# The delta rule's small substitution on GpSimd instead of VectorE, in a hybrid decoder layer

## The chip, the cores and the metric

The kernel runs on one core of one Trainium2 chip. A core has five engines that take their instructions in order and wait for one another by semaphores: TensorE (PE; its weight loads are shown apart as PEld), VectorE (DVE), ScalarE (ACT), GpSimd (POOL) and SyncE (SP), which here issues nearly all transfers. The metric is the time of one execution on the device in microseconds, as the median of several runs. The median before is 2311.64 us.

## The reference, cut to what matters

One decoder layer on 1,024 tokens of width 1,024, in float32: a gated feed-forward layer, a mixer of eight gated delta-rule heads (head dimension 128) beside sixteen state-space heads, a second feed-forward layer, and a last norm. The change lies in the delta rule. There the reference solves a unit lower triangular system for each chunk:

```python
def gated_delta_rule(q, k, v, g, beta):
    ...
    kk = jnp.einsum("bhcld,bhcsd->bhcls", k, k)
    a_low = jnp.where(strict, beta[..., :, None] * kk * decay, 0.0)
    t_inv = lax.linalg.triangular_solve(
        eye + a_low, jnp.broadcast_to(eye, a_low.shape),
        left_side=True, lower=True, unit_diagonal=True)
    u = jnp.einsum("bhcls,bhcsd->bhcld", t_inv, v * beta[..., None])
    w = jnp.einsum("bhcls,bhcsd->bhcld", t_inv, k * (beta * jnp.exp(gc))[..., None])
    ...
```

Everything else (projections, convolutions, gates, the state that is carried from chunk to chunk) is as usual for such layers.

## The kernel before, in words

The kernel keeps full float32 accuracy on TensorE by splitting each large operand into a high and a low part and making three products (`mm3`, L121 to L123). The feed-forward layers use a one-level Strassen scheme (L332 to L334 for the first two matrices, L551 to L553 for the third). Between them stands the mixer: first the state-space heads in four units, then the eight delta-rule heads in the loop `for h in range(GH)`, then the output projection.

One pass of that loop works on 1,024 tokens as 8 blocks of 128:

- Two weight tiles of 256 columns (loaded at L147 and L148, split at L136 and L137) give q, k, v and z by projections of 24 matmuls per half (`proj_half`, three PSUM banks tagged `pj`). `conv_silu` writes each projection to the single buffer `pre`, whose first three columns GpSimd sets to zero (L775), and VectorE adds three taps (L783).
- The decay `dt` is loaded, masked by GpSimd (`causal`, L894) and exponentiated by ScalarE. TensorE makes kk and qk (L1140, L1141), and VectorE scales them into `u` and `dt` (L1144 to L1154).
- `u` is 8 blocks of 128 by 128. Its diagonal blocks of 32 by 32, 32 of them, go to DRAM (L1160) and come back as `fu` (L1194), one small block per partition, four times over, so that each of 128 partitions holds one block and a quarter of its right-hand sides. `fx` starts as that quarter of the identity (GpSimd, L1198 and L1200).
- The substitution runs over 31 columns. For column j, L1204 multiplies up to eight entries of the solution with the rest of the row into `ft`, and L1206 subtracts `ft` from `fx`. That makes 62 instructions of 8 to 76 elements per partition, each of which needs the one before.
- `fx` goes to DRAM (L1209) and comes back transposed into `lv` (L1216) and onto the diagonal of `u` (L1217). A VectorE transpose (L1218) follows, then TensorE builds the inverse of the 64 and the 128 blocks from the small ones (L1224 to L1250). GpSimd clears a part of the buffer for that (L1235). `fu`, `fx`, `ft` and `lv` have one buffer each; the tile of L1235 shares the buffer of `fu`.
- The recurrence goes through the 8 blocks: TensorE (L1273, L1278, L1283, L1284, L1287) and VectorE (`rr` L1275, `vn` L1280, `sn` L1292) in turn, ScalarE takes the outputs (L1295). The results are normalised (L1301 to L1305) and stored to `mix_scr` (L1306).

The source writes one head after the other. The order on each engine is laid by the framework (Tile) when the kernel is built, by its own estimates of how long each instruction takes; on the chip each engine keeps that order. So in the trace the projections of one head stand between the matmuls of the recurrence of the head before, and the substitution's instructions stand between VectorE's other work. SyncE's queue of transfers and GpSimd's queue are ordered in the same way.

After the loop the output projection adds four groups of state-space rows (`group_tile`, L1340 and L1342) and then two pairs of delta-rule groups (`pair_tile`). The first groups are prepared and multiplied while the last head is still at work.

The lines of the substitution:

```python
            for j in range(31):
                r, n = j // 4 + 1, 31 - j
                t = ft[:, 0:r * n].rearrange("p (s l) -> p s l", l=n)
                V.tensor_tensor(out=t, in0=fx[:, 0:r, j:j + 1].to_broadcast([P, r, n]),
                                in1=fu[:, j:j + 1, j + 1:32].to_broadcast([P, r, n]), op=ALU.mult)
                V.tensor_tensor(out=fx[:, 0:r, j + 1:32], in0=fx[:, 0:r, j + 1:32], in1=t, op=ALU.subtract)
```

`V` is VectorE, `A` ScalarE, `G` GpSimd and `T` TensorE.

Of the kernel before, what the change touches and what calls it, by code (L numbers as in the profile page):

```python
# [16 lines left out]
ALU = mybir.AluOpType  # L17
# [4 lines left out]
P = 128  # L22
# [22 lines left out]
def kernel(  # L45
# [7 lines left out]
    V, A, G, T = nc.vector, nc.scalar, nc.gpsimd, nc.tensor  # L53
# [755 lines left out]
    with tc.tile_pool(name="gtmp", bufs=1, side="right", reuse_waits="tile") as tp:  # L809
# [23 lines left out]
        for b in range(NB):  # L833
# [12 lines left out]
                        in1=bias.unsqueeze(1).to_broadcast([P, NB, NG]), op=ALU.add)  # L846
# [11 lines left out]
        for c in (15, 13, 11, 9, 7, 5, 3):  # L858
# [8 lines left out]
                               in1=alog.unsqueeze(1).to_broadcast([P, NB, NG]),  # L867
# [11 lines left out]
                        op=ALU.subtract)  # L879
# [19 lines left out]
    for un in range(4):  # L899
# [37 lines left out]
        for b0 in range(0, NB, 2):  # L937
# [6 lines left out]
            for name, lst, sc in (("xdt", xdts, bc2(dtn, b0)), ("xe", xes, bc2(dxe, b0))):  # L944
                t = s1.tile([P, 2, 256], F32, name=name, tag=name, bufs=4)
                last_x = V.tensor_tensor(out=t.rearrange("p i (h c) -> p i h c", h=4), in0=ptv, in1=sc,
                                         op=ALU.mult)
# [42 lines left out]
        for b0 in range(0, NB, 4):  # L990
# [33 lines left out]
            for b, py, *_ in pairs:  # L1024
                for j in range(2):
                    xv = xst[j][:, b * P:(b + 2) * P]
                    V.scalar_tensor_tensor(out=xv, in0=xv, scalar=dcol[:, 2 * un + j:2 * un + j + 1],
                                           in1=py[:, j * 256:(j + 1) * 256], op0=ALU.mult, op1=ALU.add)
# [71 lines left out]
    with ExitStack() as cg:  # L1100
        g1 = cg.enter_context(tc.tile_pool(name="gdn1", bufs=1, reuse_waits="tile"))
        g2 = cg.enter_context(tc.tile_pool(name="gdn2", bufs=2, reuse_waits="tile"))
        for h in range(GH):
# [31 lines left out]
            for b0 in range(0, NB, 2):  # L1135
# [14 lines left out]
                for i in range(2):  # L1150
# [4 lines left out]
                                in0=pg.rearrange("p (i c) -> p i c", i=2)[:, :, P:2 * P],  # L1155
                                in1=dt[:, b2], op=ALU.mult)
# [24 lines left out]
            for half in range(2):  # L1181
                pt = psum("mx")
                for i in range(4):
# [4 lines left out]
                                in1=rin[:, hb].unsqueeze(2).to_broadcast([P, 4, P]), op=ALU.mult)  # L1188
# [6 lines left out]
            fx = g1.tile([P, 8, 32], F32, name="fx")  # L1195
# [5 lines left out]
            for j in range(31):  # L1201
                r, n = j // 4 + 1, 31 - j
                t = ft[:, 0:r * n].rearrange("p (s l) -> p s l", l=n)
                V.tensor_tensor(out=t, in0=fx[:, 0:r, j:j + 1].to_broadcast([P, r, n]),  # L1204
                                in1=fu[:, j:j + 1, j + 1:32].to_broadcast([P, r, n]), op=ALU.mult)
                V.tensor_tensor(out=fx[:, 0:r, j + 1:32], in0=fx[:, 0:r, j + 1:32], in1=t, op=ALU.subtract)  # L1206
            fs_q = fs_x.rearrange("j b (i q) l -> q (j b) i l", q=4)
            for q in range(4):
                nc.sync.dma_start(out=fs_q[q], in_=fx[32 * q:32 * q + 32])  # L1209
# [47 lines left out]
            for half in range(2):  # L1257
                pt = psum("sc")
                for i in range(4):
# [4 lines left out]
                                in1=wend[:, hb, h:h + 1].to_broadcast([P, 4, P]), op=ALU.mult)  # L1264
# [3 lines left out]
            for b in range(NB):  # L1268
                bs = slice(b * P, (b + 1) * P)
                rr = vr[:, b]  # L1270
                if st is not None:
# [4 lines left out]
                                           in1=vr[:, b], op0=ALU.mult, op1=ALU.add)  # L1276
# [8 lines left out]
                if b < NB - 1:  # L1285
# [5 lines left out]
                    else:  # L1291
                        V.scalar_tensor_tensor(out=sn, in0=st, scalar=egt[:, b, h:h + 1],  # L1292
                                               in1=p3[:, 0:P], op0=ALU.mult, op1=ALU.add)
# [191 lines left out]
```

## Time and profile before

| | |
|---|---|
| median of 3 runs | 2311.64 us (2310.7 to 2312.34) |
| the profiled execution | 2312.76 us, of which the span of the profile is 2310.9 us |
| granted TensorE clock | 0.998 |
| HBM traffic | 211.55 MB read, 67.73 MB written, 121 GB/s over the span |
| GpSimd in the whole kernel | 53.5 us busy, 125 instructions |

A row of a group of instructions reads: line, engine, operation, output tile <- input tiles, shapes, count, then busy time and mean nanoseconds of one, then the idle time of the engine before them and what ended it. A row in order of time begins with the start and the length. A row of waits reads: who waited <- for whom, total us, times, the longest. A row of stages reads: the stretch, its length, then busy us and instructions of PE, PEld, DVE, ACT and POOL, the granted clock, the share of the DMA engines and GB/s.

### The profile page before, as it was taken

The page shows a single profiled execution, that of the slowest core. Times are in us where ns is not written, and L with a number is a line of the kernel's source. Part 1 is how long each engine was busy: PE and PEld are TensorE (multiplying, and loading weights), DVE is VectorE, ACT ScalarE, POOL GpSimd, SP SyncE. Part 2 cuts the span into 40 slices and gives each one's busy share as a digit, 9 for nine tenths or more (in the row PEclk, how much of TensorE's full clock was granted, in tenths as well). Part 3 has the DMA queues.
Part 4 walks back from the last instruction along what each step waited for, and adds up shares of the span by engine and source line. Part 5 has one row for each costly group of instructions (what it writes and reads, how often), then busy time and mean ns, then how long its engine had stood idle before and what let it go on. Part 6 is the DMA issues. An engine that isn't in the chain of part 4 may idle for free.

```text
span 2310.9 us, 31493 instructions
## 1 busy us (share of the span) xinstructions
PE 2279.0 (99%) x11766; PEld 1871.6 (81%) x11766; DVE 1726.6 (75%) x3349; ACT 1097.1 (47%) x1990; POOL 53.5 (2%) x125
## 2 busy tenths in 40 slices
PE   7999999999999999999999999999999999999998
PEld 5788888888878888888888888888878888888886
DVE  7977776767765675678778888778698777767787
ACT  7433333343467785864455556422543333334344
POOL 0000000000000100000000000000000000000000
PEclk9999999999999999999999999999999999999999
DMA  3333332573652222222333222335223333329446
GB/s 111 126 113 104 105 107 99 177 278 128 222 182 75 92 92 72 73 88 74 83 101 82 73 82 61 116 98 192 91 74 123 110 104 106 105 89 356 139 154 214
DMA packets 220957, 281.33 MB, mean 122 GB/s; under 512 B 47008, under 2 KB 153564, under 8 KB 219780
## 3 DMA queue, kind: packets, MB, share of 16 engines
q1 hardware_dynamic: 220548, 279.23, 36.8%
q8 instruction: 92, 1.51, 0.3%
q14 instruction: 61, 0.50, 0.1%
q0 software_dynamic: 256, 0.10, 0.0%
HBM read 211.55 MB, written 67.73 MB: 121 GB/s over the span
## 4 chain that ended last, share of the span: by engine, by line
PE 91%; DVE 4%; ACT 3%; issue 1%; DMA 1%; SPq 0%; POOL 0%; DVEq 0%; ACTq 0%
PE ps_pj L123 10%; PE ps_pj L121 10%; PE ps_pj L122 10%; PE ps_pj L334 6%; PE ps_pj L332 6%; PE ps_pj L333 6%; PE ps_mx L332 3%; PE ps_mx L333 3%; PE ps_mx L334 3%; PE ps_pj L552 2%; PE ps_pj L553 2%; PE ps_pj L551 2%; PE ps_oo L334 2%; PE ps_oo L333 2%; PE ps_oo L332 2%; PE ps_sc L551 1%
## 5 line engine op out<-in xcount | busy, mean ns | idle before, releaser
L123 PE MATMUL ps_pj<-hhi,wlo 128*128 128x512 f32 x832 | 334.9, 403 | 0.0
L121 PE MATMUL ps_pj<-hhi,whi 128*128 128x512 f32 x832 | 333.3, 401 | 0.4 <-ACT gsb L825 0.4
L122 PE MATMUL ps_pj<-hlo,whi 128*128 128x512 f32 x832 | 332.5, 400 | 0.0
L332 PE MATMUL ps_pj<-bh,ah 128*128 128x512 f32 x688 | 268.3, 391 | 3.0 <-ACT ah L239 1.6
L334 PE MATMUL ps_pj<-bh,al 128*128 128x512 f32 x688 | 268.8, 391 | 0.5 <-DVE al L240 0.5
L333 PE MATMUL ps_pj<-bl,ah 128*128 128x512 f32 x688 | 268.4, 390 | 0.0
L121 PEld LDWEIGHTS ps_pj<-hhi,whi 128*128 128x128 f32 x832 | 157.2, 189 | 28.7 <-ACT gsb L825 0.9
L123 PEld LDWEIGHTS ps_pj<-hhi,wlo 128*128 128x128 f32 x832 | 157.1, 189 | 28.6 <-issue 0.7
L122 PEld LDWEIGHTS ps_pj<-hlo,whi 128*128 128x128 f32 x832 | 157.0, 189 | 28.1
L332 PEld LDWEIGHTS ps_pj<-bh,ah 128*128 128x128 f32 x688 | 129.4, 188 | 30.9 <-ACT m L341 2.1
L239 ACT CAST ah<-wst 128x512 fp32r<-128x512 f32 x88 | 54.6, 622 | 209.1 <-PE ps_oo L333 124.3
L239 ACT CAST hid<-hraw 128x1024 fp32r<-128x1024 f32 (+1 forms) x84 | 82.3, 981 | 149.2 <-PE ps_oo L553 56.0
L334 PEld LDWEIGHTS ps_pj<-bh,al 128*128 128x128 f32 x688 | 129.6, 188 | 27.5 <-DVE al L240 0.9
L333 PEld LDWEIGHTS ps_pj<-bl,ah 128*128 128x128 f32 x688 | 129.6, 188 | 27.3 <-DVE bl L240 0.4
L315 DVE TENSOR_TENSOR as<-wst 128x512 f32<-128x512 f32 x220 | 145.0, 683 | 1.9 <-DMA wst<-in_ffn_w_up_dram 1.5
L240 DVE TENSOR_TENSOR al<-as,ah 128x512 fp32r<-128x512 f32 x220 | 140.9, 684 | 4.3 <-ACT ah L239 4.0
L332 PE MATMUL ps_mx<-bh,ah 128*128 128x512 f32 x352 | 138.3, 395 | 2.4 <-ACT bh L239 0.9
L333 PE MATMUL ps_mx<-bl,ah 128*128 128x512 f32 x352 | 138.4, 393 | 0.4 <-DVE bl L240 0.4
L334 PE MATMUL ps_mx<-bh,al 128*128 128x512 f32 x352 | 137.6, 391 | 0.0
L239 ACT CAST ah<-as 128x512 fp32r<-128x512 f32 x220 | 124.9, 618 | 19.2 <-DVE as L315 19.1
L240 DVE TENSOR_TENSOR hid<-hraw,hid 128x1024 fp32r<-128x1024 f32 (+1 forms) x84 | 95.0, 1131 | 33.7 <-ACT hid L239 33.0
L341 ACT COPY m<-ps_pj 128x512 f32<-128x512 f32 x88 | 51.6, 589 | 124.3 <-PE ps_pj L334 122.2
(448 smaller groups left out, 5116.7 us busy)
## 6 DMA issues: line engine op xcount, KB each, us to landing
hraw<-hid_scr SPq DMA_DIRECT2D x70, 512.0 KB, 4.3
hid_scr<-hs SPq DMA_DIRECT2D x110, 256.0 KB, 2.2
wst<-in_ffn_w_down_dram SPq DMA_DIRECT2D x50, 512.0 KB, 4.6
wst<-in_ffn_w_gate_dram SPq DMA_DIRECT2D x22, 1024.0 KB, 5.5
wst<-in_ffn_w_up_dram SPq DMA_DIRECT2D x22, 1024.0 KB, 5.2
wst<-in_w_in_dram SPq DMA_DIRECT2D x36, 512.0 KB, 5.1
hid_scr<-sg SPq DMA_DIRECT2D x44, 256.0 KB, 2.0
keep<-in_ffn_w_down_dram SPq DMA_DIRECT2D x20, 512.0 KB, 6.2
```

The source lines that it names most:

```text
L121: T.matmul(o, lhsT=wh, rhs=mh, start=first, stop=False)
L122: T.matmul(o, lhsT=wh, rhs=ml, start=False, stop=False)
L123: T.matmul(o, lhsT=wl, rhs=mh, start=False, stop=last)
L239: return (A.copy(out=hi, in_=src), V.tensor_tensor(out=lo, in0=src, in1=hi.bitcast(F32), op=ALU.subtract))
L240: V.tensor_tensor(out=lo, in0=src, in1=hi.bitcast(F32), op=ALU.subtract))
L315: V.tensor_tensor(out=t, in0=v[0], in1=v[1], op=v[2])
L332: T.matmul(bank, lhsT=wh[:, k], rhs=bh[:, k], start=a, stop=False, skip_group_check=True)
L333: T.matmul(bank, lhsT=wh[:, k], rhs=bl[:, k], start=False, stop=False, skip_group_check=True)
L334: T.matmul(bank, lhsT=wl[:, k], rhs=bh[:, k], start=False, stop=z, skip_group_check=True)
L341: A.copy(out=t, in_=bank)
L551: T.matmul(bank, lhsT=hh, rhs=wh, start=first and k == 0, stop=False, skip_group_check=True)
L552: T.matmul(bank, lhsT=hh, rhs=wl, start=False, stop=False, skip_group_check=True)
```

## The change

The two instructions of each step of the substitution are given to GpSimd. Operands, shapes, buffers and the number of instructions stay; the neighbours of the loop stay where they were.

```diff
             for j in range(31):
                 r, n = j // 4 + 1, 31 - j
                 t = ft[:, 0:r * n].rearrange("p (s l) -> p s l", l=n)
-                V.tensor_tensor(out=t, in0=fx[:, 0:r, j:j + 1].to_broadcast([P, r, n]),
+                G.tensor_tensor(out=t, in0=fx[:, 0:r, j:j + 1].to_broadcast([P, r, n]),
                                 in1=fu[:, j:j + 1, j + 1:32].to_broadcast([P, r, n]), op=ALU.mult)
-                V.tensor_tensor(out=fx[:, 0:r, j + 1:32], in0=fx[:, 0:r, j + 1:32], in1=t, op=ALU.subtract)
+                G.tensor_tensor(out=fx[:, 0:r, j + 1:32], in0=fx[:, 0:r, j + 1:32], in1=t, op=ALU.subtract)
```

## The prediction

> **What bounds the kernel now.** I read the page first, then the table by stage, then the waits of the mixer, then the order of time around one substitution.
>
> ```profile
> span 2310.9 us, 31493 instructions
> PE 2279.0 (99%) x11766; PEld 1871.6 (81%) x11766; DVE 1726.6 (75%) x3349; ACT 1097.1 (47%) x1990; POOL 53.5 (2%) x125
> ...
> PE 91%; DVE 4%; ACT 3%; issue 1%; DMA 1%; SPq 0%; POOL 0%; DVEq 0%; ACTq 0%
> ```
>
> TensorE is busy 99% of the span and is 91% of the chain that ended last. The eight heads of the delta rule lie between 976 and 1560 us (columns: length, then busy time of each engine with its count, granted clock, DMA share):
>
> ```profile
> 976.00:1560.00 584.00, 582.10 (x3808) 476.85 (x3803) 462.39 (x1437) 293.43 (x660) 24.08 (x79) 1.00 0.31 86
> ...
> PEld ps_oo L1284 <- DVE vn L1280: 8.6, 44, 0.4
> PEld ps_sc L1278 <- DVE rr L1275: 8.0, 41, 0.3
> PEld ps_sc L1273 <- DVE sn L1292: 7.4, 37, 0.4
> ...
> PEld ps_sc L1224 <- DVE lv L1218: 1.0, 3, 0.4
> ```
>
> Of 584.0 us TensorE is busy 582.1, so 1.9 us are open. The finer waits are weight loads held up by VectorE's recurrence results: 8.6 + 8.0 + 7.4 = 24.0 us in 122 waits of some 0.2 us, mostly latency from one engine to the next. L1224, the first TensorE work that uses the substitution, waits 1.0 us in all: TensorE arrives there when the data does.
>
> The moved work, all heads together:
>
> ```profile
> L1206 DVE TENSOR_TENSOR fx<-fx,ft 128x60 f32<-128x60 f32 (+24 forms) x248 | 52.5, 212 | 5.2
> L1204 DVE TENSOR_TENSOR ft<-fx,fu 128x60 f32<-128x60 f32 (+24 forms) x248 | 51.8, 209 | 5.4
> ```
>
> VectorE loses 104.3 us, 13.0 per head. It isn't the bound, so that is no time by itself. What counts is when the substitution ends. One head in order of time (start, length):
>
> ```profile
> 1201.64 1.71 SPq L1194 DMA_DIRECT2D fu<-fs_u  x4
> DMA to landing us min/median/max: 2.2/2.6/2.9
> 1212.34 0.18 DVE L1204 TENSOR_TENSOR ft<-fx,fu 128x31 f32<-128x31 f32 x1
> 1241.84 0.17 DVE L1206 TENSOR_TENSOR fx<-fx,ft 128x8 f32<-128x8 f32 x1
> 1242.08 2.53 SPq L1209 DMA_DIRECT2D fs_x<-fx  x4
> 1249.00 0.45 SPq L1216 DMA_DIRECT2D lv<-fs_x  x1
> 1252.71 0.45 DVE L1218 STREAM_TRANSPOSE lv<-lv 128x256 f32<-128x256 f32 x1
> 1253.55 0.21 PE L1224 MATMUL ps_sc<-lv,u 32*32 32x32 f32 x1
> 1259.80 1.14 PE L1250 MATMUL ps_sc<-u,lv 64*64 64x64 f32 x16
> 1268.16 1.70 SPq L1194 DMA_DIRECT2D fu<-fs_u  x4
> ```
>
> The last of four loads of `fu` is issued near 1202.9 and lands 2.6 us later, at 1205.5. VectorE gets to the substitution at 1212.3, since the recurrence of the head before and the convolution come first, and ends at 1242.0: 36.5 us after the data. Then come the trip through DRAM (L1209, L1216), the transpose at 1252.7 and TensorE at 1253.6. The last L1216, landing like the L1209 and L1194 transfers some 1.8 to 2.6 us after its issue, is there near 1250.8, so about 1.9 us are spare. The substitution may therefore take 36.5 + 1.9 = 38.4 us from the landing without TensorE noticing, if its order stays.
>
> **The change part by part.** Removed from VectorE: 62 instructions per head. Added to GpSimd: the same 62, each needing the one before. The loop gives 1,560 elements per row for each of the two kinds, a mean of 50 per instruction. The trace has no GpSimd instruction with two inputs; the nearest rows:
>
> ```profile
> L1200 POOL MEMSET fx<- 32x8 f32 x32 | 3.4, 106 | 1.8
> L82 POOL TENSOR_SCALAR_AFFINE_SELECT triu<-triu 128x128 f32<-128x128 f32 x1 | 0.3, 296 | 0.0
> ...
> 906.37 1.10 POOL L894 TENSOR_SCALAR_AFFINE_SELECT md<-md 128x1024 f32<-128x1024 f32 x1 [28.96 <-ACT cte L975]
> 977.78 0.58 POOL L1200 MEMSET fx<- 32x8 f32 x4
> ```
>
> A select of 128 elements takes 0.296 us and one of 1,024 takes 1.10, so 0.90 ns per element on a fixed 0.18 us. Four memsets of 0.106 take 0.58, so some 0.05 us lie between two instructions. At 50 elements a one-input instruction would cost 0.18 + 0.045 + 0.05 = 0.28 us: the low end, 17.4 us per head. Two inputs at twice the price make 0.45 + 0.05 = 0.50: the high end, 31.0 us. Neither is nearer, so I take the middle, 0.39 us, 24.2 us per head.
>
> The Trainium skill, GPSIMD Engine Reference, section "Elementwise — side-by-side cycle accounting", speaks against the change: a two-input instruction takes 1.96 times VectorE's time there (for 2,048 elements). By that, as an estimate, 62 instructions at 0.21 us become 25.5 us. No run here shows it yet.
>
> GpSimd doesn't run alone. In the trace:
>
> ```profile
> 1228.88 0.16 DVE L118 SCALAR_TENSOR_TENSOR co<-rs_t,co 128x8 f32<-128x8 f32 x1
> 1230.43 1.27 DVE L783 SCALAR_TENSOR_TENSOR kt<-pre,cols,kt 128x1024 f32<-128x1024 f32 x1
> 1230.66 2.00 POOL L894 TENSOR_SCALAR_AFFINE_SELECT dt<-dt 128x1024 f32<-128x1024 f32 x1 [16.68 <-PE ps_pj L123]
> 1231.63 1.05 DVE L118 SCALAR_TENSOR_TENSOR co<-rs_t,co 128x8 f32<-128x8 f32 x1
> ```
>
> The select issued during a convolution tap lasts 2.00 us instead of 1.10, and the tiny L118 behind the tap lasts 1.05 instead of 0.16, to the end of the select: they take turns. The Trainium skill, SBUF — State Buffer, section "Who interferes with whom", states it as a rule: a VectorE instruction with two SBUF inputs and a GpSimd instruction that reads SBUF block one another for the whole instruction. By that rule, the trace agrees.
>
> So each large VectorE instruction with two SBUF inputs stands in the way of the chain. Between the landing and the present end:
>
> ```profile
> L783 DVE SCALAR_TENSOR_TENSOR qt<-pre,cols,qt 128x1024 f32<-128x1024 f32 x3 | 3.8, 1281 | 0.5 <-ACT qt L781 0.5
> L783 DVE SCALAR_TENSOR_TENSOR kt<-pre,cols,kt 128x1024 f32<-128x1024 f32 x3 | 3.8, 1275 | 0.0
> L783 DVE SCALAR_TENSOR_TENSOR vt__10675<-pre,cols,vt__10675 128x1024 f32<-128x1024 f32 x2 | 2.6, 1282 | 0.0
> L137 DVE TENSOR_TENSOR wlo<-wst,whi 128x1024 fp32r<-128x1024 f32 x2 | 2.4, 1221 | 0.0
> ...
> L1305 DVE TENSOR_TENSOR vr<-vr,co 128x1024 f32<-128x1024 f32 x1 | 1.2, 1217 | 0.0
> L1129 DVE TENSOR_TENSOR qe<-qe,qt 128x1024 f32<-128x1024 f32 x1 | 1.2, 1216 | 0.0
> ```
>
> They sum to 3.8 + 3.8 + 2.6 + 2.4 + 1.2 + 1.2 = 15.0 us. GpSimd's own select and two memsets add 1.3. The recurrence's rr, vn and sn read PSUM for one input; I cost the collision there at nothing, and if that fails each of some 22 results per head waits up to 0.39 us, 8.6 us per head.
>
> With the present order of the other engines the substitution takes 24.2 + 15.0 + 1.3 = 40.5 us from the landing and ends at 1246.0, 4.0 us later than now. Less 1.9 spare, TensorE waits 2.1 us per head, 16.8 us over eight. From the ends of the price: 17.4 us and no collision end at 1224.2, early, at no cost; 31.0 us with all collisions end at 1252.8, and 8.9 us in eight heads make 71 us.
>
> But the order will be laid anew at build time, by prices I don't know. If the new order counts the 24.2 + 1.3 us of GpSimd and nothing of the turns, it expects the end near 1231 and lays L1224 and what follows 11 us earlier. Up to there VectorE's taps for q and k and one `wlo` (3.8 + 3.8 + 1.2 = 8.8 us) stand in the way; the chain is 8.8 us late, 6.9 beyond the spare, and TensorE, strictly in its order, waits that long in seven heads: 48.3 us. (The last head has fewer such instructions ahead of it.) I take the middle of 16.8 and 48.3, 32.6 us.
>
> Other queues. SyncE's L1209 now waits for GpSimd; behind it stand L1216, L1217, the store of `zc` and a load of weights:
>
> ```profile
> 1250.53 0.39 SPq L147 DMA_DIRECT2D wst<-in_w_in_dram  x1
> ...
> 1289.31 1.04 ACT L136 CAST whi<-wst 128x1024 fp32r<-128x1024 f32 x1
> ```
>
> These weights are split 38 us after their issue, so some us of delay there are hidden. On GpSimd the memsets of `pre` (L775) and the select (L894) stand among the 62; one instruction of 0.39 us ahead of them is hidden, because three `pj` banks hold two half projections of 24 matmuls ahead. L1235 need not wait for VectorE any more; nothing waited for it. The buffer `fu`, single, is held from 1201.6 to 1260.9 and refilled at 1268.2: 7.2 us of slack, so the ring bites only beyond 43.7 us.
>
> What it may gain: part of the 24.0 us of small waits and the 1.9 us open. The 62 instructions are mixed into only the later part of each recurrence; I take 4 us, at most 6 with the open time, as the bound, and 2 us as likely.
>
> The sum against the profiled execution: 2310.9 span and 1.9 around it are 2312.76 us; 2312.8 + 32.6 = 2345.4. The median of the runs is 1.1 us below that execution, so 2344.
>
> **The rivals.** First, on the other side: GpSimd is in time. It starts 6.8 us earlier than VectorE does (1205.5 against 1212.3). At 38.4 us or less from landing to end, or if the new order lays L1224 later by what GpSimd needs, TensorE just works on something else: its work is the same and there is always another head's projection. At 0.28 us an instruction, 17.4 + 15.0 + 1.3 = 33.7 us is in time. For it: the 99%, and TensorE's order that meets its data within 1.0 us today, so the order's prices are good for VectorE. Against it:
>
> ```profile
> ACT dt L1128 <- POOL dt L894: 6.1, 4, 2.4
> ```
>
> ScalarE waits for GpSimd's select in four heads, 6.1 us: where GpSimd is in the chain today, the order comes out too early. Result 2306 to 2313, likeliest 2310.
>
> Second, far slower: the order prices a GpSimd instruction like VectorE's, 0.24 us from start to start, 15 us per head, and expects the end at 1220.5. The chip needs 24.2 + 8.8 = 33 us, to 1238.5; 18.0 late, 16.1 beyond the spare, in seven heads 113 us: 2425. The memsets of `pre` would then also be late by more than the banks hide. It decides as soon as the expected price is under two thirds of the real one.
>
> **How the numbers follow.** A measurement of this kernel tells about 0.2%, 4.6 us, from no change. The forecast (a few us lost per head) gets 0.50; GpSimd in time 0.37, of which 0.07 gains more than 4.6 us and 0.30 stays within; the far slower case 0.13. So faster 0.07, same 0.30, slower 0.63. The range runs from 2308, inside the in-time case, to 2400, above the 71 us of the dear end; it leaves out part of the gain and the far slower case. The forecast's own range is 2315 to 2383.
>
> **What would show it.** Right: L1204 and L1206 on POOL at 0.3 to 0.5 us, with lengths above 1 us where a tap or `wlo` runs; waits of PEld at L1224 (or of L1218 for its load) of 2 to 7 us per head; TensorE's busy share in 976 to 1560 falling to some 95%; VectorE's busy time down by about 104 us. Wrong: L1224 without waits and the stage as long as now (in time); POOL instructions under 0.28 or over 0.50 us without a collision; waits of rr, vn or sn on POOL; a loss outside the eight heads.

## The result, and the profile after

The changed kernel takes 2466.19 us (median of 5 runs, 2462.11 to 2469.53), the kernel before on the same chip 2311.75 us. The ratio is 1.0664, with a 95% interval of 1.0652 to 1.0676: 154 us slower, where the prediction had said 32 us and at most 88. The profiled execution took 2466.19 us; its span is 2464.5 us.

The page of the changed kernel, engines and the chain that ended last:

```profile
PE 2329.3 (95%) x11766; PEld 1910.8 (78%) x11766; DVE 1647.7 (67%) x2853; ACT 1080.7 (44%) x1980; POOL 247.4 (10%) x621
...
PE 72%; POOL 8%; DVE 8%; DMA 5%; issue 3%; ACT 3%; SPq 2%; POOLq 0%; DVEq 0%; ACTq 0%
```

TensorE still has 11,766 instructions. Of the 153.6 us by which the span grew, 103.3 are idle TensorE (135.2 us idle against 31.9), and 50.3 are TensorE being busy for longer with the same work. TensorE's share of the last chain fell from 91% to 72%; GpSimd, VectorE and transfers take 21% of it, against 5% before.

The stages (same columns as before), before the heads, in them and after them:

```profile
0.00:976.00 976.00, 957.57 (x4671) 785.98 (x4672) 698.07 (x1031) 510.02 (x868) 29.80 (x48) 1.00 0.39 127
976.00:1713.00 737.00, 632.58 (x3788) 516.05 (x3787) 383.79 (x951) 278.08 (x653) 217.59 (x575) 0.87 0.25 71
1713.00:2464.50 751.50, 739.11 (x3310) 608.72 (x3309) 565.81 (x872) 292.59 (x460) 0.00 (x0) 1.00 0.42 140
```

The whole loss is in the heads: they take 737 us instead of 584, at a granted clock of 0.87 instead of 1.00. The two other stages are as long as they were. In the waits, two things stand out:

```profile
PE ps_sc L1224 <- DVE lv L1218: 87.8, 8, 13.4
DVE vt__8521 L783 <- POOL pre L775: 15.4, 1, 15.4
```

L1224 waited 1.0 us in all; now TensorE stands there in every head, some 11 us at a time. And in seven heads the taps of v wait 8 to 15 us (the longest is shown) for the memset of `pre`, which stands behind the 62 instructions on GpSimd.

Counted from the landing of its data, the substitution does not end later. One head in order of time (start, length), with the beginning of the next:

```profile
1167.07 0.39 PE L1140 MATMUL ps_mx<-kt 128*128 128x128 f32 x2
1189.25 0.24 POOL L1204 TENSOR_TENSOR ft<-fx,fu 128x31 f32<-128x31 f32 x1 [44.47 <-DMA fu<-fs_u]
1193.99 1.15 POOL L1206 TENSOR_TENSOR fx<-fx,ft 128x52 f32<-128x52 f32 x1
1198.53 0.29 POOL L1206 TENSOR_TENSOR fx<-fx,ft 128x48 f32<-128x48 f32 x1
1221.78 0.21 POOL L1206 TENSOR_TENSOR fx<-fx,ft 128x8 f32<-128x8 f32 x1
1222.02 2.52 SPq L1209 DMA_DIRECT2D fs_x<-fx  x4
1222.30 3.93 DVE L783 SCALAR_TENSOR_TENSOR vt__9957<-pre,cols,vt__9957 128x1024 f32<-128x1024 f32 x3 [12.44 <-POOL pre L775]
1232.80 0.45 DVE L1218 STREAM_TRANSPOSE lv<-lv 128x256 f32<-128x256 f32 x1 [6.58 <-DMA lv<-fs_x]
1233.30 0.26 PE L1224 MATMUL ps_sc<-lv,u 32*32 32x32 f32 x1 [11.62 <-DVE lv L1218]
1251.96 0.38 PE L1140 MATMUL ps_mx<-kt 128*128 128x128 f32 x2
1267.07 1.81 SPq L1160 DMA_DIRECT2D fs_u<-u  x4
1274.78 0.24 POOL L1204 TENSOR_TENSOR ft<-fx,fu 128x31 f32<-128x31 f32 x1 [47.69 <-DMA fu<-fs_u]
1307.07 0.21 POOL L1206 TENSOR_TENSOR fx<-fx,ft 128x8 f32<-128x8 f32 x1
1318.45 0.26 PE L1224 MATMUL ps_sc<-lv,u 32*32 32x32 f32 x1 [11.49 <-DVE lv L1218]
```

From the landing of `fu` to the end of the last L1206 it takes 32.7 us (1189.25 to 1221.99). With VectorE it took 36.5, since VectorE began 6.8 us after the landing; the 62 instructions alone took 29.7 there, so GpSimd is 3 us longer on them and still ends sooner. What changed is what lies around it. In the kernel before, TensorE started the kk products (L1140) of this head and of the next one here:

```profile
1182.49 0.38 PE L1140 MATMUL ps_mx<-kt 128*128 128x128 f32 x2
1246.79 0.38 PE L1140 MATMUL ps_mx<-kt 128*128 128x128 f32 x2
```

The second is 6.8 us ahead of L1224 (1253.55), and five of the next head's eight kk products come ahead of it. After the change none does: the first L1140 comes 18.7 us behind L1224 (1251.96 against 1233.30). So the heads have become one ring, in which the next substitution cannot begin until the one before is used: L1224 to the next kk product 18.7 us, to the store of `u` 15.1, to the first L1204 7.7, the 62 instructions 32.5, transfers to L1224 11.2. The sum is 85.2 us, the distance of two L1224 (1233.30 to 1318.45); before it was 63.2 (1253.55 to 1316.79).

The clock, in four short stretches of that head:

```profile
1222.00:1224.00 2.00, 0.00 (x0) 0.00 (x0) 1.67 (x2) 0.00 (x0) 0.26 (x2) 0.88 0.14 21
1226.00:1228.00 2.00, 0.00 (x0) 0.00 (x0) 0.22 (x1) 1.06 (x1) 0.83 (x6) 0.50 0.92 256
1248.00:1252.00 4.00, 4.00 (x19) 3.49 (x18) 1.33 (x3) 0.50 (x3) 0.00 (x0) 0.65 0.00 0
1252.00:1256.00 4.00, 4.00 (x30) 3.69 (x29) 3.30 (x8) 3.15 (x8) 0.00 (x0) 1.00 0.33 133
```

TensorE stopped near 1221.7 and went on at 1233.3. The clock fell to 0.50 in the pause and was back at 1.00 near 1250.8 (that is what a mean of 0.65 from 1248 to 1252 says), after 17.5 us of work at half speed. Over the eight heads this stretch is 8 to 18 us long, 122 us together. If all of that work ran twice as fast at the full clock, half of it, 61 us, would be extra time; 50.3 us of longer busy time were found, with the same instructions.

### The profile page after: what moved, and what is told of

Same layout as the page of the kernel before. It is cut to its first block, busy times and chain, and to the rows that moved or that the text cites. A ratio compares the mean times of both kernels' runs of the same rounds, so it can differ in the third digit from the quotient of the medians.

```text
span 2464.5 us, 31445 instructions
## 1 busy us (share of the span) xinstructions
PE 2329.3 (95%) x11766; PEld 1910.8 (78%) x11766; DVE 1647.7 (67%) x2853; ACT 1080.7 (44%) x1980; POOL 247.4 (10%) x621
## 4 chain that ended last, share of the span: by engine, by line
PE 72%; POOL 8%; DVE 8%; DMA 5%; issue 3%; ACT 3%; SPq 2%; POOLq 0%; DVEq 0%; ACTq 0%
PE ps_pj L123 7%; PE ps_pj L122 7%; PE ps_pj L121 7%; PE ps_pj L332 6%; PE ps_pj L334 6%; PE ps_pj L333 6%; POOL fx L1206 4%; POOL ft L1204 3%; PE ps_mx L332 3%; PE ps_mx L333 3%; PE ps_mx L334 3%; DMA wst<-in_ffn_w_down_dram 2%; PE ps_pj L552 2%; PE ps_pj L553 2%; PE ps_pj L551 1%
## 5 line engine op out<-in xcount | busy, mean ns | idle before, releaser
L121 PE MATMUL ps_pj<-hhi,whi 128*128 128x512 f32 x832 | 342.4, 412 | 15.6 <-ACT vt__11393 L781 3.2
L123 PE MATMUL ps_pj<-hhi,wlo 128*128 128x512 f32 x832 | 344.4, 414 | 0.0
L122 PE MATMUL ps_pj<-hlo,whi 128*128 128x512 f32 x832 | 340.7, 410 | 0.0
L121 PEld LDWEIGHTS ps_pj<-hhi,whi 128*128 128x128 f32 x832 | 162.2, 195 | 48.1 <-ACT vt__11393 L781 3.6
L1204 POOL TENSOR_TENSOR ft<-fx,fu 128x60 f32<-128x60 f32 (+24 forms) x248 | 98.2, 396 | 337.3 <-DMA fu<-fs_u 318.5
```

What stands on the lines that cost most here:

```text
L121: T.matmul(o, lhsT=wh, rhs=mh, start=first, stop=False)
L122: T.matmul(o, lhsT=wh, rhs=ml, start=False, stop=False)
L123: T.matmul(o, lhsT=wl, rhs=mh, start=False, stop=last)
L1204: G.tensor_tensor(out=t, in0=fx[:, 0:r, j:j + 1].to_broadcast([P, r, n]), in1=fu[:, j:j + 1, j + 1:32].to_broadcast([P, r, n]), op=ALU.mult)
```

## The experiments

Two theories. **Order and queues**: GpSimd is fast enough; the loss comes from what the build-time order puts behind the substitution, on TensorE and in the queues of GpSimd, SP and ScalarE. **Speed**: 62 dependent instructions on GpSimd, in turns with VectorE, are too long for a head in any order. Each run below has the range that its theory gave beforehand. The table gives every run; the period is a quarter of the distance between the first substitution instruction of heads 3 and 7 of the eight, the length is that from the first of the 62 to the end of the last, as the median of those heads; both in us, from one profile each.

| run | us | ratio to before (95%) | period | length | clock |
|---|---|---|---|---|---|
| before | 2312 | | 63.3 | 28.4 | 0.998 |
| changed kernel | 2466.2 | 1.065 to 1.068 | 84.6 | 32.5 | 0.960 |
| e3_pre_on_vector | 2469.7 | 1.066 to 1.070 | 84.4 | 32.2 | 0.959 |
| e4_no_taps | 2436.8 | 1.051 to 1.056 | 78.9 | 26.5 | 0.966 |
| e7_longer_pre_vector | 2468.5 | 1.064 to 1.070 | 83.2 | 48.2 | 0.970 |
| e1_late2 | 2423.6 | 1.046 to 1.050 | 78.4 | 28.4 | 0.979 |
| e2_late1 | 2420.5 | 1.044 to 1.049 | 77.3 | 29.6 | 0.975 |
| e5_late1_pre_vector | 2420.5 | 1.045 to 1.049 | 77.3 | 29.3 | 0.977 |
| e8_late2_pre_vector_dt | 2436.4 | 1.050 to 1.058 | 81.2 | 30.2 | 0.971 |
| e9_uncoupled | 2393.0 | 1.033 to 1.037 | 73.2 | 27.3 | 0.981 |
| e11_queues_open | 2344.4 | 1.013 to 1.016 | 65.7 | 33.1 | 0.993 |
| e6_v_late1 | 2313.8 | 0.999 to 1.001 | 64.1 | 31.0 | 0.999 |
| e10_uncoupled_vector | 2313.5 | 1.000 to 1.002 | 64.4 | 24.2 | 0.999 |
| e12_queues_open_vector | 2312.2 | 0.999 to 1.001 | 65.0 | 31.2 | 0.999 |

**e1_late2 and e2_late1: TensorE's order moved later.** The loop body becomes a generator, and what follows the substitution of a head is traced behind the first part of the next head (e2), or behind the first convolution of the head after that (e1). A `yield` lets the source of another head come in between. The diff is e2's, whose two `yield`s stand ahead of `fs_x` and ahead of `lv`; e1 has a third one behind the first convolution, and an order edge (`issue_after`) that makes the framework lay the rest of a head behind a given instruction.

```diff
-        for h in range(GH):
+        def head(h):
...
+            yield
...
+        for h in range(GH):
+            next(heads[h])
+            if h:
+                next(heads[h - 1], None)
+            next(heads[h])
```

> GpSimd substitution, with the source rearranged so that each head's work behind the substitution (from L1218 on) is laid on TensorE behind the first half of the q projection two heads later: the number of projection matmuls ahead of the second head's L1224 goes from 1513 to 1584 (1548 before the change). Order theory (the loss is TensorE reaching L1224 some 11 us before the data, and the slow clock after that wait): waits at L1224 under 10 us in all, clock at 0.99 or more, time 2305 to 2325. Rival 'GpSimd is too slow' (chain and turns themselves cost the time): the same 62 instructions and the same turns, time stays above 2400. Rival 'queue' (the memsets of pre stand behind the chain and hold up the convolution of v): the 8 to 15 us waits of the taps for pre stay, time 2340 to 2400.

> The same rearrangement with less shift: the work behind the substitution is traced just after the next head's first part, which puts the second head's L1224 behind 1536 projection matmuls instead of 1513 (23 x 0.227 = 5 us, and some kk and qk matmuls). Order theory: waits of 3 to 6 us per head instead of 11, time 2360 to 2410, between the change and e1_late2. Rival 'GpSimd is too slow': above 2440, since nothing of GpSimd's work changes.

e1 ran 99 us above the range of the order theory, into the one given for a GpSimd that is too slow; e2 ran 10 us above its range. The wait at L1224 did go (two heads of eight are left with it), but others took its place. e1, waits:

```profile
PE ps_mx L1147 <- DVE jd L1151: 66.2, 12, 9.4
ACT qe L1132 <- DMA dt<-g_scr: 79.5, 6, 13.8
```

e2, order of time near the end of one substitution (1196.89):

```profile
1203.77 1.06 ACT L1125 ACTIVATE qe<-dt 128x1024 f32<-128x1024 f32 x1 [14.19 <-DMA dt<-g_scr]
1212.98 0.79 PE L121 MATMUL ps_pj<-hhi,whi 128*128 128x512 f32 x1 [11.23 <-ACT vt__9712 L781]
1220.62 0.38 PE L1140 MATMUL ps_mx<-kt 128*128 128x128 f32 x2
```

TensorE now stands in the projections of v, whose banks ScalarE has not emptied, and the kk product still comes 24 us behind the end of the substitution. The ring has another link, but it is a ring. At first I took the memset of `pre`, in GpSimd's queue behind the 62, for that link, and passed over the first of these rows; e5 below shows the error.

**e3_pre_on_vector: the memset alone.** `G.memset(pre[:, 0:3], 0.0)` becomes `V.memset`.

> As the change, but the memset of pre (L775) made by VectorE, so that no convolution waits for GpSimd's queue; TensorE's order is the same as in the change. Order theory: the 11 us waits at L1224 stay (perhaps 1 us shorter, the memset no longer waiting inside the chain), only the 2 to 3 us waits of L121 for the v projection go: 2425 to 2455. Rival 'queue': most of the loss goes, below 2370.

No gain. In the order of the change the memset's lateness is not the wait that ends last; L1224 still waits, in these seven heads and 10.8 us in the other:

```profile
PE ps_sc L1224 <- DVE lv L1218: 79.9, 7, 15.1
```

**e4_no_taps: the substitution without most turns.** The three taps of the convolutions in the eight heads are left out (that part of the computation is missing).

> As the change, but the three taps of the convolutions of q, k and v are left out in the eight heads (VectorE's 1.28 us instructions with two SBUF inputs; the output is then another). About six of nine collisions of the chain go, 0.9 us each. Order theory with the turns as what the order leaves out: chain 26 to 27 us instead of 32.7, waits at L1224 of 4 to 6 us per head, time 2370 to 2410. Order theory with an underpriced single instruction: waits stay at 9 to 11 us, time above 2430.

```profile
1184.41 0.24 POOL L1204 TENSOR_TENSOR ft<-fx,fu 128x31 f32<-128x31 f32 x1 [4.06 <-DMA fu<-fs_u]
1208.30 0.21 POOL L1206 TENSOR_TENSOR fx<-fx,ft 128x8 f32<-128x8 f32 x1
```

Here the 62 take 24.1 us in the same head, 8.6 us less than the 32.7 above. Two of them still last 1.33 and 1.15 us beside a large VectorE instruction, so the turns are worth some 10 us a head and not only 8.6. With most of them gone, 29 us of the 154 go (some of it because the convolutions are shorter too), and L1224 still waits 76.7 us in eight heads. So the turns are not the main cause. Of the two branches of the expectation it is the second that came true, the time above 2430 us and waits of 9 to 11 us a head (9.6 here): it speaks for an order that counts too little for a single GpSimd instruction, though no run shows the order's own prices.

**e7_longer_pre_vector: a longer chain.** An idle memset of 336 columns goes ahead of each L1204 on GpSimd. (The memset of `pre` stays on GpSimd, whatever the label says.)

```diff
+                G.memset(ft, 0.0)
                 G.tensor_tensor(out=t, in0=fx[:, 0:r, j:j + 1].to_broadcast([P, r, n]),
```

> The changed kernel with an idle memset of 336 columns ahead of each product on GpSimd and the memset of pre left where it is. The chain gets some 31 x 0.35 = 11 us longer, and the order made at build time, which counts it, lays TensorE's work behind the substitution 23 to 36 projection matmuls later. Theory (TensorE's order is laid for too short a chain, and what is behind the substitution then stands in front of the next head's kk product): period of a head = kk product to the end of the wait (23 + 43 + 11 = 77 us) and almost nothing ahead of the next kk product, 78 us against 84.5 now: about 2415 to 2440 us, faster than the changed kernel although the chain is longer. Rival (the length of the chain alone sets the period): 8 x 11 us more, 2540 to 2570 us.

Both ranges were missed, but the pair of numbers says much: the substitution is 16 us longer and the kernel no slower. One head, from the first kk product of the next:

```profile
1319.42 0.38 PE L1140 MATMUL ps_mx<-kt 128*128 128x128 f32 x2
1331.60 0.26 PE L1225 MATMUL ps_sc<-lv,u 32*32 32x32 f32 x1 [8.31 <-DVE lv L1219]
1348.42 1.81 SPq L1160 DMA_DIRECT2D fs_u<-u  x4
```

The order, which counts the memsets, lays three of the next head's eight kk products ahead of the inverse (L1225) and five behind it. From the first matmul of the inverse to the next store of `u` it is 16.8 us (1331.60 to 1348.42), against 33.8 in the change (1233.30 to 1267.07). So the order takes 17.0 us out of the ring, about what the longer chain puts in (47.7 us for the substitution that follows against 32.5). The expectation had the chain 5 us too short, and 23 us from the first kk product to the substitution where it is 37 (1319.42 to 1356.72), since the wait now stands in the middle of the kk products. The length of the substitution alone does not set the time.

The clock came back sooner here, after 4.5 us of work behind the wait of 8.31 us:

```profile
1331.60:1336.00 4.40, 4.40 (x41) 3.21 (x41) 3.43 (x12) 0.81 (x2) 0.00 (x0) 0.50 0.61 186
1336.20:1340.00 3.80, 3.80 (x75) 3.23 (x74) 1.45 (x7) 1.23 (x3) 0.00 (x0) 1.00 0.53 134
```

**e5_late1_pre_vector and e6_v_late1.** e2 with the memset of `pre` on VectorE, and the rearranged order of e2 with the substitution on VectorE.

> This joins two edits that each failed alone: the work behind a head's substitution is laid on TensorE behind the next head's projections (as in e2_late1), and the memset of pre is made by VectorE, so that the convolution of v no longer queues on GpSimd behind the 62 instructions. Theory (the loop): in e2_late1 the period of a head, some 78 us, is a loop: chain end, memset of pre, convolution of v, first kk product of the next head, products and both transfers (24 us), chain (30 us). With the memset on VectorE that loop is cut; what is left is kk product to first matmul behind the substitution, 24 + 30 + 12 = 66 us, against about 64 us of TensorE's own work in the head. Then 2315 to 2345 us, waits of TensorE on ps_pj below 2 us a head, and a granted clock above 0.985. Rival (GpSimd's 62 instructions are simply too slow for a head, whatever the order): 2400 to 2425 us, with the wait moved to a third place.

> Control: the rearranged trace order of e2_late1 with the substitution still on VectorE. Every theory expects that the rearrangement alone moves little: 2305 to 2325 us. If it comes out near 2400, the loss of e2_late1 is the rearrangement's and not GpSimd's.

The control came out as before: the rearrangement is free. e5 gained nothing on e2 and lies in the range given for the rival; the trace shows the next link. The queue of SP, ScalarE and TensorE in one head (the substitution ends at 1200.50):

```profile
1200.53 2.54 SPq L1210 DMA_DIRECT2D fs_x<-fx  x4
1203.17 0.54 SPq L1124 DMA_DIRECT2D dt<-g_scr  x1
1207.10 1.06 ACT L1125 ACTIVATE qe<-dt 128x1024 f32<-128x1024 f32 x1 [14.13 <-DMA dt<-g_scr]
1216.31 0.80 PE L121 MATMUL ps_pj<-hhi,whi 128*128 128x512 f32 x1 [11.17 <-ACT vt__9712 L781]
```

SP issues in order: the store of `fx` waits for GpSimd, and the load of the next head's decay stands behind it. ScalarE, in order too, stands 14 us at the exponential of that decay, with the copies that free TensorE's banks behind it.

**e8_late2_pre_vector_dt.** The order of e1, the memset on VectorE, and the decay's load and exponentials traced ahead of the substitution.

> The later order of e1_late2 (the work behind the substitution of head h stands behind the first convolution of head h+2's projections), the memset of pre on VectorE, and the load of dt with its exponentials and its select issued ahead of the previous head's substitution instead of behind it, so that neither the SP queue nor GpSimd's queue holds the decay matrix until the chain has ended. Theory (the loop): no loop of more than about 64 us a head is left, so 2300 to 2325 us, clock above 0.99, waits behind the substitution only in the last two heads (13 us together as in e1_late2). Rival (GpSimd too slow in any order): 2400 us or more.

This one, too, landed in the rival's range. The load was traced earlier and still laid behind the store on SP. The likely reason is that its tile has two buffers and in this order the second comes free late; no run shows that alone:

```profile
1210.50 2.54 SPq L1226 DMA_DIRECT2D fs_x<-fx  x4
1216.92 0.45 SPq L1116 DMA_DIRECT2D dt<-g_scr  x1
```

**e9_uncoupled and e10_uncoupled_vector.** e5 with the decay's load on ScalarE's queue, its mask added by VectorE, and order edges that hold the work behind the substitution, on VectorE and on TensorE, until the next head's v is through; e10 is the same with the 62 on VectorE.

```diff
-            nc.sync.dma_start(out=dt, in_=g_scr[h]...)
+            nc.scalar.dma_start(out=dt, in_=g_scr[h]...)
-            causal(dt, (NB,))
+            causal_v(dt)
...
+                with tc.issue_after(ends[h][0].ins), tc.issue_after(ends[h][1].ins):
+                    next(heads[h - 1], None)
```

> GpSimd makes the substitution as in the change, and everything that the earlier runs showed waiting behind it in a queue is taken out of that queue: the memset of pre on VectorE; dt's load on ScalarE's queue instead of SP's (where it stood behind the store that waits for the end of the substitution), and its mask added by VectorE instead of selected by GpSimd; the work behind the substitution of head h traced behind the first part of head h+1 and held there by two order edges (on VectorE behind the taps of v, on TensorE behind the transposes of v). Theory (the loss is coupling through the queues that the order puts in front of the long chain, not GpSimd's speed): the slowest loop left is kk product to kk product through the chain, below TensorE's own 64 us a head, so 2300 to 2335 us, clock above 0.99, no wait of more than 3 us a head on TensorE in heads 1 to 6. Rival (GpSimd's chain with its two transfers does not fit a head in any order): 2380 us or more, with waits of 8 to 12 us a head on TensorE.

> The same program as e9_uncoupled with the 62 instructions on VectorE: what the rearrangement alone is worth, and with e9 beside it what the engine alone is worth in an order that suits both. Theory: 2300 to 2335 us, and within 10 us of e9_uncoupled, a little slower if VectorE's 104 us of additional work are felt. Rival (GpSimd itself is the loss): e10 near 2312 us and e9 more than 70 us above it.

e10 is as fast as before. e9 is 73 us better than the change, but 80 above its control, and by the ranges stated beforehand both runs spoke for the speed theory (2380 us or more; more than 70 us apart). The trace of e9 shows what still hangs on the substitution (it ends at 1193.36):

```profile
1199.97 0.33 ACTq L1120 DMA_DIRECT2D dt<-g_scr  x1
1200.35 0.31 ACT L1323 ACTIVATE jk<-vr 128x128 bf16<-128x128 f32 x1 [9.61 <-DMA u<-fs_x]
1200.78 0.17 DVE L1324 SCALAR_TENSOR_TENSOR sso<-sso,cq 128x8 f32<-128x8 f32 x1 [10.89 <-ACT jk L1323]
1210.20 0.79 PE L1159 MATMUL ps_mx<-kt 128*128 128x128 f32 x2 [6.14 <-DVE jd L1163]
```

The load on ScalarE's queue was issued only when a transfer behind the substitution had landed (why it waited for that one, the rows don't say). ScalarE stood 9.6 us with it, VectorE 10.9 us behind ScalarE, and TensorE 6.1 us behind VectorE. VectorE's transpose of `lv`, which needs the same data, also stands ahead of its work for the kk products, but in six of the eight heads VectorE did not wait for it; it waited 23.7 us in the other two.

**e11_queues_open and e12_queues_open_vector.** Both are taken out together: an order edge puts the decay's load, back on SP, ahead of the store of `fx`, with a third buffer, and a second one puts the transpose behind VectorE's last work for the kk products. For space, `lv` loses its unused quarter and `rr` and `vn` have one buffer each.

```diff
+            with tc.issue_after(decays[min(h + 1, GH - 1)][2].ins):
+                for q in range(4):
+                    nc.sync.dma_start(out=fs_q[q], in_=fx[32 * q:32 * q + 32])
```

> e9_uncoupled with the two couplings that its trace still shows taken out: dt's load of the next head is ordered on SP's queue ahead of the store that waits for the end of the substitution (in e9_uncoupled it came about 6 us behind the end of the substitution, although it was issued from ScalarE's queue), with a third buffer of dt and qe so that it can go (for space lv loses its unused quarter and rr and vn have one buffer each); and VectorE's transpose of lv is ordered behind all that VectorE does for the next head's kk products, not only behind the taps of v. Theory (coupling through queues): nothing of head h+1 up to its own fu load stands behind head h's substitution any more, so TensorE's own 64 us a head set the period: 2300 to 2330 us, clock above 0.99, TensorE's waits below 2 us a head in heads 1 to 6. Rival (GpSimd's chain cannot be fitted): 2370 us or more.

> The same source as e11_queues_open with the 62 instructions on VectorE. Theory: within 15 us of before, 2305 to 2330 us; e11 beside it gives what GpSimd for VectorE is worth when nothing waits in a queue behind the substitution: within 10 us of each other. Rival: e11 more than 50 us above this one.

e11 is 14 us above the range of the order theory, 26 below the rival's (2370 us or more), and 32 above its control, where 10 had been expected. It is 122 us faster than the change: 79% of the loss is gone, with the substitution still on GpSimd and nothing changed in its 62 instructions. One head of it, SP's queue, then TensorE and GpSimd:

```profile
1214.13 0.42 SPq L1119 DMA_DIRECT2D dt<-g_scr  x1
1216.90 0.24 POOL L1227 TENSOR_TENSOR ft<-fx,fu 128x31 f32<-128x31 f32 x1 [29.68 <-DMA fu<-fs_u]
1249.59 0.38 PE L1158 MATMUL ps_mx<-kt 128*128 128x128 f32 x2
1249.62 0.21 POOL L1229 TENSOR_TENSOR fx<-fx,ft 128x8 f32<-128x8 f32 x1
1249.86 2.53 SPq L1233 DMA_DIRECT2D fs_x<-fx  x4
```

The substitution takes 32.9 us, as long as in the changed kernel, but the next kk product starts as it ends and no longer 30 us later; the period is 65.7 us. Of the 32 us that are left, the waits of TensorE in the heads name most:

```profile
PE ps_mx L1158 <- DVE jd L1162: 11.6, 1, 11.6
PE ps_sc L1249 <- DVE rs_t L116: 9.1, 1, 9.1
PE ps_mx L1203 <- DVE vr L1205: 6.6, 5, 2.3
```

The first two, 20.7 us, are single waits in the last head, at its kk products and at its inverse; behind the second there is no next head to work on. In heads 3 to 7 the period is 65.7 us against 65.0 in the control, so in those heads the chain on GpSimd, 33.1 us long, fits. That, and not the ranges that e1, e5, e8 and e9 fell into, is what refutes the speed theory. No version with GpSimd beat the kernel before, and the same rearrangements with VectorE (e6, e10, e12) are level with it: TensorE sets the pace there, so a lighter VectorE had little to win.

## Why the prediction was wrong

- **The bound.** Right: TensorE, idle for 1.9 us of the 584 in the heads, and all of the loss lies in the eight heads.
- **The price of an instruction.** Near: 0.39 us was taken, the middle of two bounds because neither was nearer, so some of this is luck. Where no large VectorE instruction is in the way, the changed kernel shows 0.28 to 0.42 us from start to start, 0.36 in the mean, which makes 22.2 us a head. The Trainium skill, GPSIMD Engine Reference, section "Elementwise — side-by-side cycle accounting", had led to an estimate of 25.5 us a head; the trace nearly agrees, with 24.1 in e4's head, two collisions included.
- **The turns.** Right in kind, too dear: 15.0 us taken and 1.3 for GpSimd's own small work; 32.7 less 22.2 leaves 10.5 us for both. Nine instructions of the head above last 1.15 to 1.36 us and not some 0.3; each collision costs about 0.9 us, less than the whole length of VectorE's instruction (1.2 to 1.3), and the order put ten of those beside the chain and not twelve. The collision with rr, vn and sn, costed at nothing, was nothing: in the changed kernel they hardly meet the chain, but in e2, e9 and e11 they run beside it, and GpSimd's instructions next to them alone last at most 0.34 us. So the chain is 32.7 us, not 40.5, and GpSimd was in time by the prediction's own test of 38.4 us with the old order.
- **The step that failed: the new order and what a wait in it costs.** The prediction had the right clause ("lays L1224 and what follows 11 us earlier"), costed the lateness at 6.9 us and then took the middle with the case of an unchanged order, without a reason for the middle. The order was laid some 16 us earlier, seen from the kk product: TensorE reaches L1224 54.6 us after it (1167.07 to 1221.68) instead of 71.1 (1182.49 to 1253.55), and the wait is 11.6 us. Worse, a wait there was treated as a loss by itself. In the new order L1224 of one head stands ahead of the kk product of the next, so the wait delays the start of the next substitution, and the heads run one after the other, at 85.2 us and not 63.2. "There is always another head's projection" was no longer true: TensorE keeps its order and could not get to it.
- **The other queues.** The prediction hid the memset of `pre` behind three banks and a load of weights on SP behind 38 us; it did not name the decay's load. The memset did no harm that a run shows (e3, and e5 beside e2). The decay's load did, as soon as TensorE's order was mended: it was the next link in the traces of e1, e5, e8 and e9.
- **The clock.** Not in the sum at all; it is 50 of the 154 us. The Trainium skill, TensorE: Matmul & The Clock Gate, section "Part 1: The HAM clock gate (the "warmup" mystery)", says that an idle window of about 3.4 us halves the clock and that about 3.4 us of sustained work restores it. The clock does halve in the rows above, but sooner, 1.8 us after TensorE stopped (by the 0.88 from 1222 to 1224). The way back took 8 to 18 us in the changed kernel, which does not agree, and 4.5 us in the rows of e7, which nearly does; the measurement decides, and what makes the difference no run isolates.
- **The rivals.** The far slower case, at 0.13, was the nearest: its condition, that the order expects under two thirds of the real time, is about met (TensorE's arrival at L1224 fits an end of the chain 11 us earlier, 22 of 33 us); its 113 us of waits stand beside 103.3 us of idle time. With the clock it would have come within some 10 us (2425 and 50). e4 speaks for its reason, too, a GpSimd instruction priced too low: with most turns gone TensorE still came 9.6 us a head too early. The prices themselves no run shows; only the order can be seen.

What stays open: the last 32 us of e11 are named by their waits, but were not taken away one by one, and the share of the turns in them wasn't measured. Nor does a run separate the two links that e11 takes out together, or the clock's 50 us from the waits that bring them.

## What to carry to other kernels

When work moves to another engine in a program whose order is laid at build time, first find what will stand behind it in each in-order queue: the new engine's own small jobs, the transfer that waits for its result and the loads behind that transfer, and the main engine's first use of the result. Check above all whether that first use can slip in front of the work that starts the next round, since two overlapped rounds then become one serial ring, and a single 11 us wait costs 21 us a round. A wait of the tensor engine also has to be priced with the slow clock behind it, half as much again here (50.3 us on 103.3).

## What the runs showed of the hardware

- GpSimd's two-input instructions of 8 to 76 elements per partition last 0.20 to 0.34 us when nothing is in their way, with 0.08 us to the next one; VectorE's same instructions 0.21 us on average.
- A GpSimd instruction that meets a large VectorE instruction with two SBUF inputs lasts 1.13 to 1.39 us in most cases. Beside VectorE's rr, vn and sn, which read PSUM for one input, it lasts at most 0.34 us (e2, e9, e11).
- After the waits at L1224, of 7.6 to 13.4 us, the granted clock stayed at 0.50 for another 8 to 18 us of work, although TensorE was busy by the profile (11.70 of the 12 us from 1233 to 1245). After a wait of 8.31 us in e7 it was 4.5 us.
